# A conditioned hybrid decoder layer on one core: opening in a new order with a fifth weight buffer, conditioning units pinned in DVE's queue, tanh of the branch gates grouped by table

## The chip, the cores and the metric

One Trainium2 chip, and of it one core. The core has five engines with a queue each: PE (TensorE, matmuls), DVE (VectorE), ACT (ScalarE), POOL (GpSimd) and SP (SyncE, here only for issuing DMAs). Each queue runs in order; engines wait for each other by semaphores. The metric is device time in microseconds (us) of one execution, and the median of several runs is compared. A second measure is the span of one profiled execution, from which all rows come.

## What is computed

One layer of a decoder on 256 tokens of width 2048, in float32:

```python
def reference(x, c, w_ada, b_ada, norm1_g, w_in, ...):
    c_act = jax.nn.silu(c)
    mod = jnp.dot(c_act, w_ada[l]) + b_ada[l]
    shift1, scale1, gate1, shift2, scale2, gate2 = jnp.split(mod, 6, axis=-1)
    h = _modulate(_rms_norm(x, norm1_g[l]), shift1, scale1)
    proj = jnp.einsum("bsd,de->bse", h, w_in[l])
    lru_x, lru_gate, q, k, v, g_a, g_b = jnp.split(proj, split_idx, axis=-1)
    xc = _causal_depthwise_conv(lru_x, conv_w[l], conv_b[l])
    rec = _rg_lru(xc, ...)
    y_a = jnp.einsum("bsw,wd->bsd", rec * jax.nn.gelu(lru_gate, approximate=True), w_lru_out[l])
    att = _swa_sink_attention(q, k, v, attn_sinks[l], rel_bias)
    y_b = jnp.einsum("bsw,wd->bsd", att, w_attn_out[l])
    merged = jax.nn.sigmoid(g_a) * y_a + jax.nn.sigmoid(g_b) * y_b
    x = x + gate1[:, None, :] * jnp.einsum("bsd,de->bse", merged, w_out[l])
    h2 = _modulate(_rms_norm(x, norm2_g[l]), shift2, scale2)
    ff = jnp.square(jax.nn.relu(jnp.einsum("bsd,df->bsf", h2, w_ff1[l])))
    x = x + gate2[:, None, :] * jnp.einsum("bsf,fd->bsd", ff, w_ff2[l])
    return _rms_norm(x, final_g)
```

Two things matter here. The input of the first projection, h, needs the first columns of `mod`, and these need the whole conditioning vector times rows of `w_ada`. And the branch gates are sigmoids, which the kernel computes as a tanh of half the argument.

## The kernel before

**Layout.** Activations stand transposed: 16 k-tiles of 128 channels by 256 tokens. Each float32 weight tile of 1 MB (128 x 2048) is fetched by SP into one of four `raw` buffers (`RAW_BUFS`). It is used in halves of 1024 columns: ACT rounds a half to `wh` (L161), DVE computes the remainder `wl` (L163), and each operand pair is multiplied by three matmuls (L177 to L179), or two wide ones (L190, L191). There are three buffers each of `wh` and `wl` (`WH_BUFS`), so one and a half tiles are prepared ahead. A few tiles are multiplied unsplit (L206). Activation pairs, each 128 x 512 floats, come from a pool `kp` of 49 buffers: the x tiles `xs`, the split `h`, the results `res`, and later the split operands. PSUM has four banks for matmul groups (`pg`) and four for all else (`pa`).

**Conditioning.** `mod` has 96 columns of 128 channels. A unit of conditioning (`ada_unit`, L277) is one DVE instruction (L287): it multiplies a `raw` buffer of `w_ada` (1 MB, fetched by SP at L272) with the silu'd vector laid out in a line, `scr`, and sums to one column. The first 32 units are shift1 and scale1, in pairs by k-tile: two units, then `norm1_tile` (L299) makes h[j], with L301 on DVE, L303 and the rounding L146 on ACT, and the remainder L147 on DVE.

**The opening.** Token-major x is fetched in four DMAs (L99) into `wh` and `wl` buffers, `vec` (all small vectors) and the identity `idt` by ACT's queue (L91, L93). PE lays out `scr` by 16 transposes (L225), ACT copies it (L226), ACT and DVE sum squares of x (L229, L233). Then x is scaled by quarters q (`turn_in`, L252): token block 0 on DVE (L254), block 1 on ACT (L255); PE transposes it (L261), ACT copies it to `xs` (L263). Quarter q yields k-tiles 4q to 4q + 3. The order is written out by hand in L307 to L323.

**Passes.** The first projection runs in three passes (`PASSES`: k-tiles 0 to 1 and 2 to 5 for 56 features, 6 to 9 for 40), so that matmuls can begin with two k-tiles done. After each weight tile about 0.85 units of conditioning follow (`ADA_FIRST`). In pass one the results leave PSUM by ACT (L372), in the others they are added by DVE (L374, L376).

**Units.** After that, 240 loop turns (L799) each take one weight tile: the turn splits the weights of two turns ahead, issues its matmuls and what finishes them, then some steps of a list `side` (attention, LRU, gelu) by a budget, then units of conditioning by a budget. Tiles of the rest of the first projection (`in_unit`, L418) are shorter, with 6 or 10 k-tiles a feature. LRU steps come in groups of four: sigmoids (L580, L581), exp and tanh (L587, L588), sqrt (L596), each DVE work between them. The helper `table` (L465) keeps such groups apart: every activation of a group is placed behind all those of the group before, so that ACT's function tables are loaded once a group. The tanh of branch gates (L637, L640) is not among them in this version.

**What sets the order.** A planner orders the instructions on each queue by the program's order and by when it takes their inputs to be ready; an instruction later in the program can be placed earlier. `keep_in_program_order` (called `pin` in the code) ties an instruction to stand behind the last one that the program has issued on the same engine so far; it doesn't wait for that one to finish. The opening is pinned on DVE, ACT and SP, and so are the eight conditioning units 4 to 11.

Of the kernel before, what the change touches and what calls it, by code (L numbers as in the profile page):

```python
# [10 lines left out]
F32 = mybir.dt.float32  # L11
F32R = mybir.dt.float32r
AF = mybir.ActivationFunctionType
ALU = mybir.AluOpType
# [3 lines left out]
P = 128  # L18
# [8 lines left out]
F_K, F_V, F_Q, F_LX, F_LG, F_GA, F_GB = 0, 2, 4, 20, 36, 52, 68  # L27
W_IN_ORDER = (list(range(48, 50)) + list(range(50, 52)) + list(range(32, 48)) + list(range(0, 16))
              + list(range(16, 32)) + list(range(52, 68)) + list(range(68, 84)))
RAW_BUFS, WH_BUFS, WCH = 4, 3, 1024  # L30
LAG, CC, CG, CV, CS = 2, 1, .6, .3, 2.5
SSD = 4

# [7 lines left out]
PASSES = [(0, 2, 56), (2, 6, 56), (6, 10, 40)]  # L41
# [6 lines left out]
def _done(f):  # L48
# [4 lines left out]
V_BADA, V_G1, V_CW, V_CB, V_BA, V_BX, V_LAM, V_G2, V_GF, V_C, V_SINK = (  # L53
    0, 96, 112, 176, 192, 208, 224, 240, 256, 272, 288)
# [4 lines left out]
def hybrid_layer(ctx: ExitStack, tc: tile.TileContext, x, xt, wada, w_p, w_r, w_f, vec, lruw, relb,  # L59
                 onehot, maskc, ident, out):  # L60
    nc = tc.nc
    te, ve, se = nc.tensor, nc.vector, nc.scalar

    cp = ctx.enter_context(tc.tile_pool(name="cp", bufs=1))
    wp = ctx.enter_context(tc.tile_pool(name="wp", bufs=2))
    kp = ctx.enter_context(tc.tile_pool(name="kp", bufs=49))
    tp = ctx.enter_context(tc.tile_pool(name="tp", bufs=9))
    sp = ctx.enter_context(tc.tile_pool(name="sp", bufs=2))
    pg = ctx.enter_context(tc.tile_pool(name="pg", bufs=4, space=PSUM))
# [5 lines left out]
    def nm(s):  # L75
        cnt[0] += 1
        return f"{s}{cnt[0]}"

    def pair(dt=F32):
        return kp.tile([P, 2, T], dt, tag="k2", name=nm("k"))  # L80

    def tmp(shape=(P, 2, T), dt=F32):
        return tp.tile(list(shape), dt, tag="t2", name=nm("t"))

    def bank(shape):
        return pa.tile(list(shape), F32, tag="pa", name=nm("pa"))


    pin = tc.keep_in_program_order
    vc = cp.tile([P, NV], F32, name="vc")  # L90
    pin(se.dma_start(out=vc, in_=vec))  # L91
    idt = cp.tile([P, P], F32, name="idt")
    pin(se.dma_start(out=idt, in_=ident))  # L93

    xtok = {}
# [11 lines left out]
    def rstd_cols(ss, pin=lambda i: i):  # L107
        st = sp.tile([P, 8], F32, tag="st", name=nm("st"), bufs=2)
        v, s, r, q = st[:, 0:2], st[:, 2:4], st[:, 4:6], st[:, 6:8]
        pin(ve.tensor_scalar(out=v, in0=ss, scalar1=1.0 / 2048, scalar2=EPS, op0=ALU.mult, op1=ALU.add))  # L110
        pin(se.activation(s, v, AF.Sqrt))
        pin(ve.reciprocal(out=r, in_=s))

        pin(ve.scalar_tensor_tensor(out=q, in0=r, scalar=-0.5, in1=r, op0=ALU.mult, op1=ALU.mult))
        pin(ve.tensor_tensor(out=q, in0=q, in1=v, op=ALU.mult))
        pin(ve.scalar_tensor_tensor(out=r, in0=q, scalar=1.5, in1=r, op0=ALU.add, op1=ALU.mult))
        return r
# [25 lines left out]
    def split(src, pin=lambda i: i):  # L143

        hl = pair(F32R)
        pin(se.activation(hl[:, 0], src, AF.Copy))  # L146
        pin(ve.tensor_tensor(out=hl[:, 1], in0=src, in1=hl[:, 0].bitcast(F32), op=ALU.subtract))  # L147
        return hl


    def w_dma(src, n, pin=lambda i: i):
        raw = wp.tile([P, 2048], F32, tag="raw", name=nm("rw"), bufs=RAW_BUFS)
        pin(nc.sync.dma_start(out=raw[:, :n], in_=src))
        return raw, n

    def w_split(raw, n, pin=lambda i: i, o0=0):
        parts = []
        for o in range(o0, o0 + n, WCH):
            c = min(WCH, o0 + n - o)
            wh = wp.tile([P, WCH], F32R, tag="wh", name=nm("wh"), bufs=WH_BUFS)  # L160
            pin(se.activation(wh[:, :c], raw[:, o:o + c], AF.Copy))  # L161
            wl = wp.tile([P, WCH], F32R, tag="wl", name=nm("wl"), bufs=WH_BUFS)
            pin(ve.tensor_tensor(out=wl[:, :c], in0=raw[:, o:o + c], in1=wh[:, :c].bitcast(F32), op=ALU.subtract))  # L163
            parts.append((wh, wl))
        return parts

    def w_load(src, n):
        return w_split(*w_dma(src, n))
# [48 lines left out]
    scr = cp.tile([P, KT * P], F32, name="scr")  # L217
# [31 lines left out]
    rs1 = rstd_cols(ss1, pin)  # L249
    xs = []  # L250

    def turn_in(q):  # L252

        pin(ve.tensor_scalar(out=xtok[0, q], in0=xtok[0, q], scalar1=rs1[:, 0:1], scalar2=None, op0=ALU.mult))  # L254
        pin(se.activation(xtok[1, q], xtok[1, q], AF.Copy, scale=rs1[:, 1:2]))  # L255
        for j in (2 * q, 2 * q + 1):
            px = bank([P, 512])
            for i in range(2):
                for b in range(2):
                    e = (2 * (j % 2) + i) * P  # L260
                    te.transpose(px[:, i * T + b * P:i * T + (b + 1) * P], xtok[b, q][:, e:e + P], idt)  # L261
            xs.append(pair())
            pin(se.activation(xs[j].rearrange("p a b -> p (a b)"), px, AF.Copy))  # L263
# [4 lines left out]
    same = lambda i: i  # L268

    def ada_dma(pin=same):  # L270
        raw = wp.tile([P, KT * P], F32, tag="raw", name=nm("ra"), bufs=RAW_BUFS)
        pin(nc.sync.dma_start(out=raw, in_=wada[ada_next[0] + len(ada_raw)]))  # L272
        ada_raw.append(raw)

    ada_raw = []

    def ada_unit(pin=same):  # L277
        if not ada_raw:
            ada_dma()
        raw = ada_raw.pop(0)  # L280
        n = ada_next[0]
        ada_next[0] += 1
        c = ADA_ORDER[n]

        if 2 * PASSES[0][1] <= n < 2 * PASSES[0][1] + 8:
            pin = tc.keep_in_program_order
        pin(ve.tensor_tensor_reduce(out=raw, in0=raw, in1=scr, scale=1.0, scalar=vc[:, V_BADA + c:V_BADA + c + 1],  # L287
                                    op0=ALU.mult, op1=ALU.add, accum_out=mod[:, c:c + 1]))
        return n

    h = [None] * KT
    a1 = cp.tile([P, KT], F32, name="a1")

    def ada_norm1():
        n = ada_unit()
        if n % 2 == 1:
            norm1_tile(n // 2)

    def norm1_tile(j, pin=same):  # L299
        xj = xs[j // 2][:, j % 2]  # L300
        pin(ve.scalar_tensor_tensor(out=a1[:, j:j + 1], in0=mod[:, KT + j:KT + j + 1], scalar=1.0,  # L301
                                    in1=vc[:, V_G1 + j:V_G1 + j + 1], op0=ALU.add, op1=ALU.mult))
        pin(se.activation(xj, xj, AF.Identity, scale=a1[:, j:j + 1], bias=mod[:, j:j + 1]))  # L303
        h[j] = split(xj, pin)


    ada_dma(pin)  # L307
    ada_dma(pin)
    first_raw = w_dma(w_p[0], 2048, pin)
    ada_dma(pin)  # L310
    turn_in(0)
    turn_in(1)
    ada_unit(pin)
    n1 = ada_unit(pin)
    first_w = w_split(first_raw[0], WCH, pin)
    norm1_tile(n1 // 2, pin)
    ada_dma(pin)
    ada_unit(pin)
    first_w += w_split(first_raw[0], WCH, pin, WCH)
    n1 = ada_unit(pin)  # L320
    turn_in(2)
    norm1_tile(n1 // 2, pin)
    turn_in(3)  # L323


# [37 lines left out]
    res = {}  # L363
# [37 lines left out]
    while ada_next[0] < 2 * KT:  # L401
        ada_norm1()
# [12 lines left out]
    def later(cost, fn, *a):  # L415
        side.append((cost, fn, a))
# [212 lines left out]

    bg = [None]  # L630

    def branch_gate(f, ps, part):
        if part is None:
            if f % 2 == 0:
                bg[0] = pair()
            res[f] = bg[0][:, f % 2]
            se.activation(res[f], ps, AF.Tanh, scale=0.5)  # L637
        else:
            ve.tensor_tensor(out=part, in0=ps, in1=part, op=ALU.add)
            se.activation(part, part, AF.Tanh, scale=0.5)  # L640


    att, mg = {}, {}
# [135 lines left out]
    in_units(F_LX, 16, lx_fin)  # L779
    in_units(F_LG, 16, lg_fin)  # L780
    in_units(F_GA, 16, lambda f, ps, part: branch_gate(F_GA + f, ps, part))
    in_units(F_GB, 16, lambda f, ps, part: branch_gate(F_GB + f, ps, part))
    n_ya = len(units)
    n_z = n_ya + 32 + Z_FROM
# [153 lines left out]
```

## Time and profile before

| | |
|---|---|
| median of 3 runs | 1591.97 us (1588.78 to 1592.4) |
| the profiled execution, its own time | 1585.86 us |
| its span | 1584.1 us |
| PE busy | 1543.9 us (97%) |
| DVE busy | 1216.9 us (77%) |
| ACT busy | 890.9 us (56%) |
| conditioning units, L287 | 96 of 2.35 us |
| splits, L161 and L163 | 534 each |
| HBM read | 384.13 MB, 244 GB/s over the span |

The span is what the profiler sees of the core from the first to the last instruction; the execution's own time has 1.76 us around it. A busy PE doesn't say that it runs at full rate, but its idle time is real. The rows that the argument needs stand in the prediction: a table of busy time by stretch, the timeline of the opening, and the waits of PE.

### The profile page before, as it was taken

What the parts mean: (1) busy time and instruction counts of PE and PEld (TensorE: products, weight loads), DVE (VectorE), ACT (ScalarE), POOL (GpSimd) and SP (SyncE); (2) the same over time, 40 slices, a digit from 0 to 9 for tenths busy, and PEclk for the clock granted to TensorE, in tenths of its full rate; (3) what the DMA queues carried; (4) which work ended last, traced back from release to release, by engine and by line L of the source; (5) the groups of instructions that cost most, each with busy time, mean ns of one, the idle gap of its engine ahead of it and who ended that gap; (6) DMA issues with size and microseconds to landing.
All of it is one profiled execution on the core that took longest, in us unless ns stands there. A gap on an engine that the chain in (4) does not pass through costs nothing.

```text
span 1584.1 us, 24932 instructions
## 1 busy us (share of the span) xinstructions
PE 1543.9 (97%) x9812; PEld 1383.8 (87%) x9812; DVE 1216.9 (77%) x1941; ACT 890.9 (56%) x1510; POOL 0.2 (0%) x4
## 2 busy tenths in 40 slices
PE   4999999999999999999999999999999999999997
PEld 4999998899988888888889988888888888888886
DVE  5898998898989879788898877965665556655664
ACT  5733447687796564445455863356434663356553
POOL 0000000000000000000000000000000000000000
PEclk7999999999999999999999999999999999999999
DMA  8998976557767768777886666875555555555552
GB/s 324 343 341 321 337 277 210 204 181 242 282 247 291 266 240 301 283 292 288 322 313 239 229 247 249 331 256 190 194 192 189 190 186 186 186 186 188 188 188 75
DMA packets 61126, 387.90 MB, mean 245 GB/s; under 512 B 6512, under 2 KB 10960, under 8 KB 18640
## 3 DMA queue, kind: packets, MB, share of 16 engines
q1 hardware_dynamic: 55728, 380.66, 66.1%
q10 hardware_dynamic: 5280, 5.64, 1.2%
q8 instruction: 77, 1.26, 0.3%
q14 instruction: 41, 0.34, 0.1%
HBM read 384.13 MB, written 2.15 MB: 244 GB/s over the span
## 4 chain that ended last, share of the span: by engine, by line
PE 86%; DVE 5%; DMA 4%; issue 3%; ACT 2%; ACTq 0%; DVEq 0%
PE pg L191 41%; PE pg L190 20%; PE pg L179 5%; PE pg L177 5%; PE pg L178 5%; DMA ra<-in_wada_dram 3%; DVE wl L163 2%; PE pg L206 2%; PE pg L193 1%; PE pg L727 1%; PE pg L728 1%; PE pg L726 1%; DVE ra L287 1%; PE pa L532 1%; PE pa L539 1%
## 5 line engine op out<-in xcount | busy, mean ns | idle before, releaser
L191 PE MATMUL pg<-k,wh 128*128 128x512 f32 x3120 | 1076.0, 394 | 0.3 <-DVE k L147 0.3
L163 DVE TENSOR_TENSOR wl<-rw,wh 128x1024 fp32r<-128x1024 f32 (+2 forms) x534 | 628.3, 1179 | 266.1 <-ACT wh L161 259.8
L161 ACT ACTIVATE wh<-rw 128x1024 fp32r<-128x1024 f32 (+2 forms) x534 | 545.0, 1022 | 509.0 <-PE pg L191 353.3
L190 PE MATMUL pg<-k,wl 128*128 128x256 f32 x2925 | 818.9, 280 | 0.6 <-DVE wl L163 0.6
L191 PEld LDWEIGHTS pg<-k,wh 128*128 128x128 f32 x3120 | 572.6, 188 | 118.9 <-PE pg L191 0.6
L190 PEld LDWEIGHTS pg<-k,wl 128*128 128x128 f32 x2925 | 550.3, 188 | 10.4 <-DVE wl L163 0.9
L177 PE MATMUL pg<-k,wh 128*128 128x256 f32 x832 | 237.6, 287 | 7.4 <-ACT k L146 5.7
L179 PE MATMUL pg<-k,wl 128*128 128x256 f32 x832 | 233.6, 284 | 3.6 <-DVE wl L163 3.6
L287 DVE CUSTOM_DVE_ANT_0 ra<-ra,scr,vc 128x2048 f32<-128x2048 f32 x96 | 225.1, 2346 | 14.4 <-DMA ra<-in_wada_dram 14.3
L178 PE MATMUL pg<-k,wh 128*128 128x256 f32 x832 | 234.2, 282 | 0.0
L177 PEld LDWEIGHTS pg<-k,wh 128*128 128x128 f32 x832 | 157.5, 190 | 10.0 <-ACT k L146 6.5
L179 PEld LDWEIGHTS pg<-k,wl 128*128 128x128 f32 x832 | 156.5, 189 | 6.2 <-DVE wl L163 4.9
L178 PEld LDWEIGHTS pg<-k,wh 128*128 128x128 f32 x832 | 157.5, 189 | 0.7 <-issue 0.3
L754 DVE SCALAR_TENSOR_TENSOR k<-pg,mod,k 128x256 f32<-128x256 f32 x128 | 61.9, 484 | 31.7 <-PE pg L191 29.5
L743 ACT ACTIVATE t<-t 128x256 f32<-128x256 f32 x55 | 23.0, 419 | 68.0 <-DVE t L198 67.8
L193 PE MATMUL pg<-k,wl 128*128 128x256 f32 x195 | 54.7, 281 | 2.0 <-DVE wl L163 2.0
L198 DVE TENSOR_TENSOR t<-pg,t 128x256 f32<-128x256 f32 x131 | 54.8, 418 | 0.0
L197 ACT ACTIVATE t<-pg 128x256 f32<-128x256 f32 x131 | 47.8, 365 | 1.7 <-PE pg L191 1.7
L193 PEld LDWEIGHTS pg<-k,wl 128*128 128x128 f32 x195 | 36.6, 188 | 10.8 <-DVE wl L163 2.8
L727 PE MATMUL pg<-z,wh 128*128 128x256 f32 x144 | 41.0, 285 | 0.0
L726 PE MATMUL pg<-z,wh 128*128 128x258 f32 x144 | 40.7, 282 | 0.0
L728 PE MATMUL pg<-z,wl 128*128 128x258 f32 x144 | 40.6, 282 | 0.0
(161 smaller groups left out, 963.1 us busy)
## 6 DMA issues: line engine op xcount, KB each, us to landing
rw<-in_w_f_dram SPq DMA_DIRECT2D x204, 1024.0 KB, 4.8
ra<-in_wada_dram SPq DMA_DIRECT2D x96, 1024.0 KB, 6.2
rw<-in_w_p_dram SPq DMA_DIRECT2D x31, 1024.0 KB, 6.4
rw<-in_w_r_dram SPq DMA_DIRECT2D x20, 768.0 KB, 4.5
rw<-in_w_r_dram SPq DMA_DIRECT2D x16, 640.0 KB, 3.9
bt<-ud ACTq DMA_DIRECT2D x8, 512.0 KB, 4.0
lw<-in_lruw_dram SPq DMA_DIRECT2D x4, 512.0 KB, 5.9
k<-in_x_dram SPq DMA_DIRECT2D x8, 256.0 KB, 6.0
```

Source lines behind the costliest of these rows:

```text
L161: pin(se.activation(wh[:, :c], raw[:, o:o + c], AF.Copy))
L163: pin(ve.tensor_tensor(out=wl[:, :c], in0=raw[:, o:o + c], in1=wh[:, :c].bitcast(F32), op=ALU.subtract))
L177: te.matmul(ps, lhsT=wh[:, w], rhs=hl[:, 0], start=k == 0, stop=False)
L178: te.matmul(ps, lhsT=wh[:, w], rhs=hl[:, 1], start=False, stop=False)
L179: te.matmul(ps, lhsT=wl[:, w], rhs=hl[:, 0], start=False, stop=k == n - 1)
L190: te.matmul(ps[:, 0], lhsT=wl[:, w], rhs=hl[:, 0], start=False, stop=False)
L191: te.matmul(ps, lhsT=wh[:, w], rhs=hl, start=k == 0, stop=k == n - 1)
L193: te.matmul(ps[:, 0], lhsT=wl[:, w], rhs=hl[:, 0], start=False, stop=False)
L287: pin(ve.tensor_tensor_reduce(out=raw, in0=raw, in1=scr, scale=1.0, scalar=vc[:, V_BADA + c:V_BADA + c + 1], op0=ALU.mult, op1=ALU.add, ac ...
L726: te.matmul(ps, lhsT=wh[:, e], rhs=z[k][:, 0:258], start=k == 0, stop=False)
L727: te.matmul(ps[:, 0:256], lhsT=wh[:, e], rhs=z[k][:, 258:514], start=False, stop=False)
L754: ve.scalar_tensor_tensor(out=x1[f], in0=ps[:, i], scalar=mod[:, 5 * KT + f:5 * KT + f + 1], in1=x1[f], op0=ALU.mult, op1=ALU.add)
```

## The change

It has five parts. `vec` is fetched by SP, ahead of x, so that ACT's queue begins with the identity. `raw` has five buffers instead of four and `kp` 48 instead of 49. The opening has a new order: two conditioning tiles, a weight tile and two conditioning tiles are fetched; quarter 1 is scaled before the first units, but transposed only after h[0]'s rounding; the first half's rounding on ACT comes ahead of h[0], its remainder on DVE behind h[0]'s L301; and h[1] comes ahead of quarters 2 and 3. All conditioning units are pinned on DVE, not only eight. The tanh of branch gates goes through `table` in the group "exp", and that of the four gates begun in pass one is put on the side list.

```diff
-RAW_BUFS, WH_BUFS, WCH = 4, 3, 1024
+RAW_BUFS, WH_BUFS, WCH = 5, 3, 1024
...
-    kp = ctx.enter_context(tc.tile_pool(name="kp", bufs=49))
+    kp = ctx.enter_context(tc.tile_pool(name="kp", bufs=48))
...
-    pin(se.dma_start(out=vc, in_=vec))
+    pin(nc.sync.dma_start(out=vc, in_=vec))
...
+    def w_round(raw, o, c, pin=lambda i: i):
+        wh = wp.tile([P, WCH], F32R, tag="wh", name=nm("wh"), bufs=WH_BUFS)
+        pin(se.activation(wh[:, :c], raw[:, o:o + c], AF.Copy))
+        return wh
+
+    def w_rest(raw, o, c, wh, pin=lambda i: i):
+        wl = wp.tile([P, WCH], F32R, tag="wl", name=nm("wl"), bufs=WH_BUFS)
+        pin(ve.tensor_tensor(out=wl[:, :c], in0=raw[:, o:o + c], in1=wh[:, :c].bitcast(F32), op=ALU.subtract))
+        return wh, wl
...
-    def turn_in(q):
-
-        pin(ve.tensor_scalar(out=xtok[0, q], in0=xtok[0, q], scalar1=rs1[:, 0:1], scalar2=None, op0=ALU.mult))
-        pin(se.activation(xtok[1, q], xtok[1, q], AF.Copy, scale=rs1[:, 1:2]))
+    def turn_in(q, step=None):
+
+        if not step:
+            pin(ve.tensor_scalar(out=xtok[0, q], in0=xtok[0, q], scalar1=rs1[:, 0:1], scalar2=None, op0=ALU.mult))
+            pin(se.activation(xtok[1, q], xtok[1, q], AF.Copy, scale=rs1[:, 1:2]))
+        if step is False:
+            return
...
-    def ada_unit(pin=same):
+    def ada_unit():
...
-        if 2 * PASSES[0][1] <= n < 2 * PASSES[0][1] + 8:
-            pin = tc.keep_in_program_order
-        pin(ve.tensor_tensor_reduce(out=raw, in0=raw, in1=scr, scale=1.0, scalar=vc[:, V_BADA + c:V_BADA + c + 1],
+        tc.keep_in_program_order(ve.tensor_tensor_reduce(out=raw, in0=raw, in1=scr, scale=1.0, scalar=vc[:, V_BADA + c:V_BADA + c + 1],
...
         pin(se.activation(xj, xj, AF.Identity, scale=a1[:, j:j + 1], bias=mod[:, j:j + 1]))
-        h[j] = split(xj, pin)
+        h[j] = pair(F32R)
+        pin(se.activation(h[j][:, 0], xj, AF.Copy))
+
+    def norm1_rest(j, pin=same):
+        xj = xs[j // 2][:, j % 2]
+        pin(ve.tensor_tensor(out=h[j][:, 1], in0=xj, in1=h[j][:, 0].bitcast(F32), op=ALU.subtract))
...
     ada_dma(pin)
     ada_dma(pin)
     first_raw = w_dma(w_p[0], 2048, pin)
     ada_dma(pin)
+    ada_dma(pin)
     turn_in(0)
-    turn_in(1)
-    ada_unit(pin)
-    n1 = ada_unit(pin)
-    first_w = w_split(first_raw[0], WCH, pin)
-    norm1_tile(n1 // 2, pin)
-    ada_dma(pin)
-    ada_unit(pin)
+    turn_in(1, False)
+    ada_unit()
+    ada_unit()
+    whs = w_round(first_raw[0], 0, WCH, pin)
+    norm1_tile(0, pin)
+    turn_in(1, True)
+    first_w = [w_rest(first_raw[0], 0, WCH, whs, pin)]
+    norm1_rest(0, pin)
+    ada_unit()
     first_w += w_split(first_raw[0], WCH, pin, WCH)
-    n1 = ada_unit(pin)
+    ada_unit()
+    norm1_tile(1, pin)
+    norm1_rest(1, pin)
     turn_in(2)
-    norm1_tile(n1 // 2, pin)
     turn_in(3)
...
+    def gate_tanh(f):
+        table("exp", se.activation(res[f], res[f], AF.Tanh, scale=0.5))
+
...
-            se.activation(res[f], ps, AF.Tanh, scale=0.5)
+            table("exp", se.activation(res[f], ps, AF.Tanh, scale=0.5))
         else:
             ve.tensor_tensor(out=part, in0=ps, in1=part, op=ALU.add)
-            se.activation(part, part, AF.Tanh, scale=0.5)
+            later(0.4, gate_tanh, f)
```

7 lines of the change are left out of this document (2 added, 5 removed).

## The prediction

> **What bounds the kernel now.** I read the stages first: a table of busy time by stretch. Columns: stretch, its length, then busy us and instruction count of PE, PE weight load, DVE, ACT, POOL, then the granted clock, the DMA share and GB/s.
>
> ```profile
> 0.00:14.00 14.00, 4.07 (x20) 3.65 (x20) 5.50 (x22) 7.75 (x16) 0.20 (x4) 1.00 0.86 332
> 14.00:20.00 6.00, 2.86 (x14) 2.05 (x13) 5.08 (x5) 3.85 (x6) 0.00 (x0) 0.53 1.01 404
> 20.00:36.00 16.00, 8.78 (x40) 7.92 (x40) 10.30 (x14) 6.56 (x12) 0.00 (x0) 0.54 0.77 294
> 36.00:110.00 74.00, 72.34 (x551) 69.91 (x552) 62.44 (x78) 44.02 (x89) 0.00 (x0) 1.00 0.91 336
> 225.00:330.00 105.00, 101.26 (x850) 88.58 (x849) 92.37 (x317) 72.70 (x220) 0.00 (x0) 1.00 0.61 212
> 330.00:480.00 150.00, 145.38 (x1026) 136.17 (x1025) 137.04 (x236) 122.23 (x209) 0.00 (x0) 1.00 0.69 246
> 480.00:860.00 380.00, 379.01 (x2187) 332.08 (x2186) 330.08 (x497) 206.18 (x335) 0.00 (x0) 1.00 0.77 284
> 860.00:1560.00 700.00, 699.99 (x4127) 617.78 (x4126) 457.35 (x591) 373.70 (x559) 0.00 (x0) 1.00 0.58 207
> 1560.00:1584.10 24.10, 15.29 (x103) 13.54 (x101) 9.09 (x19) 7.70 (x14) 0.00 (x0) 0.87 0.25 88
> ```
>
> PE is the bound from 36 us on. Its idle time is 9.9 + 3.1 + 7.2 = 20.2 us before 36 us, 1.7 in 36:110, 3.7 in 225:330, 4.6 in 330:480, 1.0 in 480:860, nothing in 860:1560, and 8.8 at the end, which the change does not touch. So the change can take from about 30 us of idle, two thirds of it in the opening. PE's matmul work itself is not changed.
>
> Next, the timeline of all engines up to 36 us, with two pieces (the first and the transposes at 28.41) from the chain that ended last, and the issues of SP. A bracket gives the idle time before an instruction and what ended it.
>
> ```profile
> 1.17 5.71 DMA idt<-in_ident_dram
> 5.41 0.22 ACT L213 ACTIVATE sc<-vc 128x16 f32<-128x16 f32 x1 [2.48 <-DMA vc<-in_vec_dram]
> 8.21 0.69 DVE L229 CUSTOM_DVE_ANT_0 t<-wh 128x512 f32<-128x512 f32 x1 [1.16 <-DMA wh<-in_xt_dram]
> 11.56 0.16 DVE L248 TENSOR_REDUCE ss<-ssq 128x2 f32<-128x8 f32 x1 [1.41 <-ACT t L233]
> 12.99 0.88 DVE L254 TENSOR_SCALAR wh<-wh,st 128x512 f32<-128x512 f32 x2
> 16.05 2.35 DVE L287 CUSTOM_DVE_ANT_0 ra<-ra,scr,vc 128x2048 f32<-128x2048 f32 x1
> 18.25 1.05 ACT L161 ACTIVATE wh<-rw 128x1024 fp32r<-128x1024 f32 x1
> 19.34 1.23 DVE L163 TENSOR_TENSOR wl<-rw,wh 128x1024 fp32r<-128x1024 f32 x1 [0.92 <-ACT wh L161]
> 20.48 0.15 DVE L301 SCALAR_TENSOR_TENSOR a<-mod,vc 128x1 f32<-128x1 f32 x1
> 20.73 0.60 ACT L303 ACTIVATE k<-k,mod,a 128x256 f32<-128x256 f32 x1 [1.42 <-DVE a L301]
> 21.83 0.80 PE L177 MATMUL pg<-k,wh 128*128 128x256 f32 x2 [4.10 <-ACT k L146]
> 25.56 2.35 DVE L287 CUSTOM_DVE_ANT_0 ra<-ra,scr,vc 128x2048 f32<-128x2048 f32 x1
> 28.23 0.15 DVE L301 SCALAR_TENSOR_TENSOR a<-mod,vc 128x1 f32<-128x1 f32 x1
> 28.41 1.96 PE pa L261 x8
> 29.54 0.60 ACT L263 ACTIVATE k<-pa 128x512 f32<-128x512 f32 x1 [6.20 <-PE pa L261]
> 30.89 0.59 ACT L303 ACTIVATE k<-k,mod,a 128x256 f32<-128x256 f32 x1
> 31.98 1.22 PE L177 MATMUL pg<-k,wh 128*128 128x256 f32 x4 [1.62 <-ACT k L146]
> 5.78 12.99 SPq L272 DMA_DIRECT2D ra<-in_wada_dram  x3
> ```
>
> The reader is to see two late tiles. h[0] starts PE at 21.83. The second conditioning unit ends at 16.05 + 2.35 = 18.4, but L301 stands in DVE's queue behind the split weight L163 and comes only at 20.48. h[1] starts PE again at 31.98. Its L301 is done at 28.38, but ACT is held by two copies (L263) that wait for transposes, and these wait for DVE's scaling behind the fourth conditioning unit, so L303 starts at 30.89. And SP's third issue of L272 hangs for a weight buffer: the DMA share falls to 0.77 in 20:36.
>
> **The change part by part.**
>
> *The head.* vec goes to SP ahead of x, so idt is alone on ACT's queue. It is 64 KB (128 x 128 x 4 bytes) and took 5.71 us behind 176 KB of vec. If it lands 1.5 to 2.5 us earlier, PE's sixteen transposes and ACT's squares move up; the reduction at 11.56 waited 1.41 us for ACT, and x itself lands at 8.21, so 1.3 us is the most that it brings; nothing, if idt is no earlier. x's four issues each slip by one issue on SP, in a time in which nothing has landed yet. I take 1.3 us at DVE, worth 0.5 us at h[1] (below).
>
> The Trainium skill, "DMA: Bandwidth & Descriptors", section "Issuing engines are not separate DMA queues", speaks against this step: a second issuing engine saves only the issue time, since all queues share the same 16 engines. By it idt would gain only the place of one issue, well under 1 us, and the sum below would be about 0.3 us less; the 5.71 us for 64 KB, late behind 176 KB in one queue, speak for the larger value.
>
> *h[0].* L301 no longer waits for L163, and ACT rounds the first weights before the copies of the second quarter. So L301 comes at about 18.4 instead of 20.48: PE, which followed L303 by 1.1, starts 2.1 us earlier, up to 3.4 with the head. This alone brings nothing at the end: with one of two k-tiles and four PSUM banks PE runs 12 matmuls and stops again.
>
> *h[1].* On DVE, after L301 at 18.4: L163 (1.14 us to the next start, 19.34 to 20.48), L147 as PE's first matmul, by about 19.9, then a unit of 2.35 less some 0.1 that neighbours overlap, the second half's split 1.14, a unit again: L301 at 25.5 instead of 28.23. L303 now follows at once (25.7 instead of 30.89), because quarters 2 and 3 come behind it: 5.2 us. Data: SP has five buffers, so the first four units and the first weights are all issued at the start. From the stage table 4.65 MB have come by 14 us and 0.404 MB per us after; vec, idt and x are 2.34 MB and each tile 1.05 MB, so the third unit lands at about 18.7 and the fourth at 21.3, both before DVE wants them. These landings let only a part of the head's 1.3 us through, and I add 0.5: h[1] 5.7 us earlier, at about 26.3.
>
> *What moves behind it.* Quarter 2's eight transposes took 1.96 us in PE's idle time at the granted clock of 0.54; now they stand on PE's path: 1.0 us at full clock to 2.0 us at half. Its two copies (0.6 each) and a scaling on ACT also delay the next weights' rounding, which waits until quarter 3's transposes free the buffer. I charge 1.4. **Opening: 5.7 - 1.4 = 4.3 us**, bounds 2.0 (h[0]'s gain only) and 5.7.
>
> *Does it last?* DVE and ACT are shifted with PE. DMA has to be as well: 36:110 runs at 0.91. In 20:36 it left 0.23 x 16 = 3.7 us unused, for want of a buffer; the fifth fills this. So supply moves up by about as much as PE.
>
> *The fifth buffer later.* Rows of the first pass change:
>
> ```profile
> 78.16 2.00 ACT L161 ACTIVATE wh<-rw 128x1024 fp32r<-128x1024 f32 x2 [2.91 <-DMA rw<-in_w_p_dram]
> 81.87 0.38 PE L179 MATMUL pg<-k,wl 128*128 128x256 f32 x1 [0.74 <-DVE wl L163]
> ```
>
> Here a weight tile arrived late and cost PE 0.74 us (its own idle; the stretch 36:110 lost 1.7 in all). One issue slot earlier is some 2.6 us (1.05 MB at 0.404). I take 0.7 back; bounds 0 and 1.7. One activation buffer fewer (48): I count at most 48 pairs in use at the gates (16 h, 32 results), so a pair is free when its successor is asked for: nothing, but if wrong a copy waits for one matmul group.
>
> *Conditioning units pinned.* The three largest waits of PE after 110 us, with the conditioning unit on DVE that stood ahead of the awaited split each time, and for the middle one ACT's rounding of those weights:
>
> ```profile
> 359.05 2.35 DVE L287 CUSTOM_DVE_ANT_0 ra<-ra,scr,vc 128x2048 f32<-128x2048 f32 x1
> 362.60 0.39 PE L179 MATMUL pg<-k,wl 128*128 128x256 f32 x1 [1.68 <-DVE wl L163]
> 383.93 1.05 ACT L161 ACTIVATE wh<-rw 128x1024 fp32r<-128x1024 f32 x1
> 384.66 2.35 DVE L287 CUSTOM_DVE_ANT_0 ra<-ra,scr,vc 128x2048 f32<-128x2048 f32 x1
> 388.55 0.39 PE L179 MATMUL pg<-k,wl 128*128 128x256 f32 x1 [0.97 <-DVE wl L163]
> 440.78 2.35 DVE L287 CUSTOM_DVE_ANT_0 ra<-ra,scr,vc 128x2048 f32<-128x2048 f32 x1
> 444.91 0.39 PE L193 MATMUL pg<-k,wl 128*128 128x256 f32 x1 [1.97 <-DVE wl L163]
> ```
>
> At 384.98 the rounded weights were ready, but DVE had begun a unit of 2.35 us 0.3 us before. A pinned unit stands behind the last DVE instruction of its loop turn, a join or a side step that itself waits for PE or ACT, so it can no longer slip ahead there. The three waits make 1.68 + 0.97 + 1.97 = 4.6 us, PE's whole idle time in 330:480; all of it back is one bound. The other: a pin adds a wait. Behind a waiting unit stand the next weights' L163 and the joins that free PSUM, and for these PE waits. DVE is 91% busy in 330:480, so a unit of 2.35 us has to stand ahead of something: the same three waits again, 0 back, or three new ones, 4.6 lost.
>
> *Tanh by table.* In program order tanh now alternates with the last two LRU groups: I count 12 loads where the trace has 10 (below the first and the last, with two activations between), since a tanh must wait for the sqrt traced before it and the next sqrt for that tanh.
>
> ```profile
> 428.67 1.28 ACT L596 ACT_TABLE_LOAD   x1
> 429.96 0.42 ACT L596 ACTIVATE t<-t 128x256 f32<-128x256 f32 x1
> 452.47 0.41 ACT L637 ACTIVATE k<-t 128x256 f32<-128x256 f32 x1
> 477.67 1.28 ACT L637 ACT_TABLE_LOAD   x1
> ```
>
> Two loads at 1.28 are 2.6 us of ACT, which is 81% busy in 330:480; the tanh at 452.47 needed none, between sigmoids. I charge half, 1.3 us; bounds 0 and, with all eight units of that stretch held up, 8 x 1.97 = 15.8.
>
> The Trainium skill, "ScalarE: Activation LUTs", section "What ACT_TABLE_LOAD costs", puts a switch at 1.28 us and a drain of 1.38 more. By it the two loads would cost 5.3 us of ACT, and the sum would be 1.3 us worse; the row has no drain: the activation at 429.96 starts 1.29 us after the load's start.
>
> **Sum.** 4.3 + 0.7 + 4.6 - 1.3 = 8.3 us. The profiled execution is 1585.86 us (span 1584.1), so 1577.6 for such a one. The median before is 1591.97, 6.1 above it, over runs from 1588.78 to 1592.4; the terms do not depend on that, so I take the difference off the median: **1583.7 us**.
>
> **The rivals.**
>
> *Supply takes the opening back.* DMA stays at its 36:110 rate and the first late weight at 78 us lands when it did; PE, 4.3 us early, then waits longer there. For: 0.91 busy. Against: the unused 3.7 us, and the fifth buffer. Left are the later terms, 3.3 us, and little of the opening: 1588.
>
> *The pins move the waits instead of removing them.* For: DVE at 91% and short units there. Against: the row of 384.66. Left are 4.3 + 0.7 - 1.3 = 3.7 us: 1588.3.
>
> *Slower: tanh and sqrt chained to PE.* Place: the eight units at 428:478. The sqrt of each next LRU step waits for a tanh, which waits for that unit's join, and ACT's queue holds the next rounding behind it. Price: up to 1.97 us a unit, as at 444.91. It decides from four units on, where 7.9 us eat the opening and the fifth buffer and the pins bring nothing; with all eight 15.8 + 1.3 - 5.0 = 12.1 slower, with six about 8: 1600. Against: the order of the trace is already nearly that one.
>
> *More.* h[1]'s whole 5.7, all of 1.7 and 4.6, no tanh charge: 12.0 us, 1580.
>
> **How the numbers follow.** Forecast 0.48 (1581 to 1586.5), more 0.12, supply 0.14, moved waits 0.17, slower or a new wait of its size 0.09. A measurement of this kernel can tell about 0.3% (4.8 us, so 1587.2 and 1596.7) from no change. The two middle rivals lie just inside it, with a fifth of their chance beyond on the fast side, and 0.02 of the last stays within: faster 0.66, same 0.27, slower 0.07. The range is 1576 to 1592: the fast case less the 3.2 us by which the runs before spread downwards, and to the median before, so that about 0.1 is left above and less below.
>
> **What would show it.** Right: PE's first L177 at 18.5 to 19.8 and the second group at 25 to 27, DMA share above 0.9 in 20:36, idt landed before 5.4, PE idle before 36 us of 14 to 16 us; no PE wait over 1 us after a unit in 330:480. Wrong: PE waits for weights at 65 to 90 us of over 2 us in all, or more PE idle than 4.6 us in 330:480.

## The result: slower, and the profile after

The changed kernel takes 1610.06 us (median of 4 runs, 1608.37 to 1610.76), against 1590.38 us for the kernel before on the same chip: ratio 1.0123, 95% interval 1.0104 to 1.0143. The forecast was 1583.7 us, faster, with a range of 1576 to 1592.

Line numbers shift: the split pair is now L158 and L163, the narrow matmuls L183 to L185 (before L177 to L179), the unsplit ones L212 (L206), a conditioning unit L294 (L287), the last add of a pass L393 (L376), h[j]'s rounding and remainder L313 and L317 (L146, L147), its inputs L309 and L311 (L301, L303), scaling L261 and L262, transposes L270, their copies L272. First the stages, in the columns and stretches of before:

```profile
0.00:14.00 14.00, 3.81 (x17) 3.44 (x17) 5.33 (x21) 7.84 (x16) 0.20 (x4) 1.00 0.85 312
14.00:20.00 6.00, 3.85 (x16) 2.95 (x16) 5.25 (x7) 3.35 (x6) 0.00 (x0) 1.00 1.03 431
20.00:36.00 16.00, 9.15 (x45) 8.53 (x46) 11.72 (x14) 8.88 (x19) 0.00 (x0) 1.00 1.01 420
36.00:110.00 74.00, 70.15 (x526) 68.07 (x525) 57.34 (x73) 40.87 (x85) 0.00 (x0) 0.98 0.78 302
110.00:225.00 115.00, 113.13 (x897) 110.22 (x897) 106.70 (x164) 45.68 (x54) 0.00 (x0) 1.00 0.88 322
225.00:330.00 105.00, 95.19 (x785) 83.95 (x783) 84.06 (x296) 62.73 (x189) 0.00 (x0) 0.97 0.56 193
330.00:480.00 150.00, 146.11 (x1042) 134.65 (x1041) 134.29 (x242) 117.05 (x210) 0.00 (x0) 1.00 0.67 237
480.00:860.00 380.00, 376.19 (x2141) 327.71 (x2140) 329.44 (x478) 214.55 (x354) 0.00 (x0) 1.00 0.77 284
860.00:1560.00 700.00, 697.48 (x4114) 615.02 (x4114) 458.96 (x614) 370.66 (x558) 0.00 (x0) 1.00 0.59 211
```

Length less PE's busy time is its idle time. Before 36 us it fell from 20.2 to 19.2. In 36:110 it grew from 1.7 to 3.9, in 110:225 from 0.1 to 1.9, in 225:330 from 3.7 to 9.8, in 480:860 from 1.0 to 3.8, in 860:1560 from nothing to 2.5; of the stretches behind 36 us only 330:480, where the pins were to help, fell, from 4.6 to 3.9. DVE is less busy in 36:110 than before (57.3 against 62.4 us): it did not become the bound by work, it stood still more. The clock column is not to be read before 36 us: it shows 1.00 there, but the matmuls from 21.6 to 32.3 us start 0.21 us apart, as those of the kernel before did where it showed 0.54; from 35.4 us on they start 0.12 us apart.

Over the profiled execution (1609.78 us, span 1608.0) PE is also busy for longer:

```profile
PE 1554.8 (97%) x9812; PEld 1389.6 (86%) x9812; DVE 1218.7 (76%) x1941; ACT 891.9 (55%) x1512; POOL 0.2 (0%) x4
```

1554.8 against 1543.9 us, for the same matmuls. So of 23.9 us of span, 13.0 are idle PE and 10.9 are longer busy time. Of these 1.1 stand before 36 us. Behind 36 us, the share of the clock that was not granted, summed over stretches of 8 us, makes 9.5 us after and 3.2 before, so by this estimate some 6 of the 10.9 are a lower clock; the rest was not told apart. The table of waits, PE alone, 36 to 330 us (total us, times, longest), says for what PE waits; its first line for the split, before and after:

```profile
PE pg L179 <- DVE wl L163: 0.9, 2, 0.7
```

```profile
PE pg L185 <- DVE wl L163: 10.5, 6, 3.2
```

The longest but one of the six, in the timeline (start, duration, engine, line; in brackets the idle time before and what ended it):

```profile
73.60 1.99 ACT L158 ACTIVATE wh<-rw 128x1024 fp32r<-128x1024 f32 x2
73.73 0.42 DVE L317 TENSOR_TENSOR k<-k,k 128x256 fp32r<-128x256 f32 x1 [1.14 <-ACT k L313]
76.26 0.85 DVE L393 TENSOR_TENSOR k<-pg,k 128x256 f32<-128x256 f32 x2 [2.11 <-PE pg L212]
77.56 0.42 DVE L393 TENSOR_TENSOR k<-pg,k 128x256 f32<-128x256 f32 x1 [0.44 <-PE pg L212]
79.28 0.42 DVE L393 TENSOR_TENSOR k<-pg,k 128x256 f32<-128x256 f32 x1 [1.30 <-PE pg L212]
79.62 2.34 DVE L294 CUSTOM_DVE_ANT_0 ra<-ra,scr,vc 128x2048 f32<-128x2048 f32 x1
81.89 2.36 DVE L163 TENSOR_TENSOR wl<-rw,wh 128x1024 fp32r<-128x1024 f32 x2
83.17 0.39 PE L185 MATMUL pg<-k,wl 128*128 128x256 f32 x1 [2.90 <-DVE wl L163]
```

The adds L393 wait for PE, and DVE idles 2.11 + 0.44 + 1.30 = 3.9 us. The unit is pinned behind the last of them. It begins when that add is done, although the next weights had been rounded since 75.6, and their two splits stand behind it for 2.3 us. PE, which from 78.87 to 80.26 multiplied what needs only the rounded weights and now needs the remainder `wl`, waits 2.90 us. Then it runs at half rate for a while (windows of the same kernel, columns as above):

```profile
80.00:83.10 3.10, 0.26 (x2) 0.06 (x1) 3.10 (x4) 0.00 (x0) 0.00 (x0) 1.00 0.86 299
83.10:87.00 3.90, 3.83 (x20) 3.83 (x20) 1.57 (x3) 0.00 (x0) 0.00 (x0) 0.58 0.99 395
87.00:90.00 3.00, 3.00 (x26) 3.00 (x26) 2.62 (x4) 1.44 (x2) 0.00 (x0) 0.98 0.58 232
```

The granted clock is 0.58 in the 3.9 us after the wait: 20 matmuls, where at the rate of the next stretch (26 in 3.0) there would be 34. That is part of the 10.9.

### The profile page after: what moved, and what is told of

It is laid out like the page before. It is cut to its first block, busy times and chain, and to the rows that moved or that the text cites. A ratio compares the mean times of both kernels' runs of the same rounds, so it can differ in the third digit from the quotient of the medians.

```text
span 1608.0 us, 24927 instructions
## 1 busy us (share of the span) xinstructions
PE 1554.8 (97%) x9812; PEld 1389.6 (86%) x9812; DVE 1218.7 (76%) x1941; ACT 891.9 (55%) x1512; POOL 0.2 (0%) x4
## 4 chain that ended last, share of the span: by engine, by line
PE 85%; DVE 8%; ACT 3%; issue 2%; DMA 1%; SPq 0%; ACTq 0%; DVEq 0%
PE pg L197 43%; PE pg L196 21%; PE pg L185 4%; PE pg L183 4%; PE pg L184 4%; DVE ra L294 3%; DVE wl L163 3%; PE pg L212 2%; PE pg L199 1%; ACT wh L158 1%; PE pg L747 1%; PE pg L748 1%; PE pg L746 1%; DMA rw<-in_w_p_dram 1%; PE pa L556 1%
## 5 line engine op out<-in xcount | busy, mean ns | idle before, releaser
L163 DVE TENSOR_TENSOR wl<-rw,wh 128x1024 fp32r<-128x1024 f32 (+2 forms) x534 | 626.6, 1177 | 278.5 <-ACT wh L158 273.1
L158 ACT ACTIVATE wh<-rw 128x1024 fp32r<-128x1024 f32 (+2 forms) x534 | 544.3, 1022 | 526.8 <-PE pg L197 362.1
L185 PE MATMUL pg<-k,wl 128*128 128x256 f32 x832 | 236.9, 287 | 11.8 <-DVE wl L163 11.7
L183 PE MATMUL pg<-k,wh 128*128 128x256 f32 x832 | 238.9, 289 | 9.6 <-ACT k L313 6.5
L294 DVE CUSTOM_DVE_ANT_0 ra<-ra,scr,vc 128x2048 f32<-128x2048 f32 x96 | 224.6, 2341 | 0.0
L185 PEld LDWEIGHTS pg<-k,wl 128*128 128x128 f32 x832 | 159.0, 192 | 14.6 <-DVE wl L163 13.7
L183 PEld LDWEIGHTS pg<-k,wh 128*128 128x128 f32 x832 | 159.2, 192 | 13.3 <-ACT k L313 7.2
L199 PEld LDWEIGHTS pg<-k,wl 128*128 128x128 f32 x195 | 36.6, 188 | 10.9 <-DVE wl L163 2.9
```

The lines of the kernel that those rows point to most:

```text
L183: te.matmul(ps, lhsT=wh[:, w], rhs=hl[:, 0], start=k == 0, stop=False)
L185: te.matmul(ps, lhsT=wl[:, w], rhs=hl[:, 0], start=False, stop=k == n - 1)
L199: te.matmul(ps[:, 0], lhsT=wl[:, w], rhs=hl[:, 0], start=False, stop=False)
L294: tc.keep_in_program_order(ve.tensor_tensor_reduce(out=raw, in0=raw, in1=scr, scale=1.0, scalar=vc[:, V_BADA + c:V_BADA + c + 1], op0=ALU. ...
```

## The experiments

Three theories were to be told apart. *Pins*: the pinned unit can't use a gap of DVE and then stands ahead of a split. *Fifth buffer*: a planner with more buffers places units or weights elsewhere. *Tanh*: the grouped tanh chains ACT. Lines are those of the changed kernel unless another is named; each ratio is to the kernel before in the same batch.

**1. Pins taken away.** From unit 12 on none is pinned.

```diff
-        tc.keep_in_program_order(ve.tensor_tensor_reduce(out=raw, ...
+        (tc.keep_in_program_order if n < 12 else same)(ve.tensor_tensor_reduce(out=raw, ...
```

> The changed kernel with units of conditioning pinned only up to unit 11, as before the change. If the pins cost the time (a unit of 2.35 us that waits behind a join for PE and then stands ahead of the next split), the execution falls from 1610 to 1580 to 1592 us and PE's waits for wl of 1 us and more before 320 us go. If the tanh order or the opening with five buffers costs it, it stays at 1604 to 1611.

1589.34 us, 1.0010 (0.9995 to 1.0025): 1.13 of the 1.23% are gone, some 18 us. The same place in its timeline:

```profile
72.44 2.35 DVE L294 CUSTOM_DVE_ANT_0 ra<-ra,scr,vc 128x2048 f32<-128x2048 f32 x1
74.71 0.42 DVE L317 TENSOR_TENSOR k<-k,k 128x256 fp32r<-128x256 f32 x1
79.22 0.42 DVE L393 TENSOR_TENSOR k<-pg,k 128x256 f32<-128x256 f32 x1 [1.30 <-PE pg L212]
79.56 2.35 DVE L163 TENSOR_TENSOR wl<-rw,wh 128x1024 fp32r<-128x1024 f32 x2
80.83 0.39 PE L185 MATMUL pg<-k,wl 128*128 128x256 f32 x1 [0.75 <-DVE wl L163]
```

The unit went into the gap ahead of the adds, the splits follow the last add at once, and PE waits 0.75 us.

**2. The kernel before with the pins alone.**

```diff
-        if 2 * PASSES[0][1] <= n < 2 * PASSES[0][1] + 8:
+        if n >= 2 * PASSES[0][1]:
```

> The kernel before with every unit from 4 on pinned, nothing else. If the pins cost the time by themselves, 1604 to 1616 us (18 us more, and somewhat more where only four buffers hold the tiles that a waiting unit keeps). If they cost it only together with the new opening or the tanh order, 1588 to 1595.

1615.45 us, 1.0176 (1.0155 to 1.0196). Pins alone bring more than the whole loss, 26.5 us, with four buffers and the old opening. The same line of its waits, 36 to 330 us:

```profile
PE pg L179 <- DVE wl L163: 16.6, 12, 3.1
```

**3. Tanh as before** (the two `table`/`later` lines undone), and **4. tanh and pins both undone**, which leaves the opening, the fifth buffer and 48 pairs.

```diff
-            table("exp", se.activation(res[f], ps, AF.Tanh, scale=0.5))
+            se.activation(res[f], ps, AF.Tanh, scale=0.5)
...
-            later(0.4, gate_tanh, f)
+            se.activation(part, part, AF.Tanh, scale=0.5)
```

> The changed kernel with the tanh of the branch gates outside the table groups, as before the change. If the tanh chained to sqrt costs the time, 1588 to 1596 us. If the pins cost it, 1604 to 1611; of the 4 us that are lost between 330 and 600 us up to 4 may return.

1607.09 us, 1.0123 (1.0108 to 1.0139), the same ratio as with the tanh grouped: tanh is not the cause.

> New opening, five buffers, 48 pairs; pins and tanh as before the change. If the opening's 4 us last, 1583 to 1588 us. If the supply takes them back, 1588 to 1592. If the new opening or the buffers themselves upset the order on the queues, over 1595.

1591.61 us, 1.0024 (1.0012 to 1.0036). The parts that were to bring 5.0 us cost 3.8 by the ratio. Runs 7 to 9 take them apart.

**5. Where the pins cost: in the passes only, or after them only** (unit 32 is the first behind the passes).

```diff
+        (tc.keep_in_program_order if n < 2 * KT else same)(...
...
+        (tc.keep_in_program_order if n < 12 or n >= 2 * KT else same)(...
```

> The changed kernel with units pinned only while the three passes run (units 0 to 31). If each pin costs where it stands, the passes' share comes back as it was: the first attention score at 237 to 240 us, as in the changed kernel (239.3), and no further loss behind it, so 1594 to 1599 us. If the later pins alone cost the time, the first score is at 232 and the time 1587 to 1592.

> The changed kernel with units 12 to 31 free and all later ones pinned. If each pin costs where it stands, the first score is at 232 us as with no pins, and the loss of some 8 us comes between 240 and 600 us: 1596 to 1601 us. If the passes' pins alone cost the time, 1587 to 1592.

1598.08 us, 1.0056 (1.0041 to 1.0071), and 1604.31 us, 1.0096 (1.0081 to 1.0111). Against 1.0010 without late pins these are 0.46% (7 us) and 0.86% (14 us), against 18 us for all pins at once: both stages pay. In the kernel with late pins only, PE still waits 6.1 us for remainders between 36 and 330 us, in four waits. Which waits make up the rest of the late part is not shown here.

**6. Is it the join?** From unit 12 on each unit is tied behind the last split issued so far instead of behind the last DVE instruction. That last instruction is mostly a join, an add such as L393 that waits for PE's result; so the unit stays out of the way of the splits but need not wait for a join.

```diff
-        tc.keep_in_program_order(ve.tensor_tensor_reduce(out=raw, ...
+        (tc.keep_in_program_order if n < 12 else behind_split)(ve.tensor_tensor_reduce(out=raw, ...
```

> The changed kernel with each unit from 12 on tied behind the last split of weights that the program has issued (in a pass that of the same tile, later that of two turns ahead), instead of behind the last instruction on DVE, which is mostly a join that waits for PE. If the wait for the join is the cost, nearly all comes back: 1584 to 1593 us. If any tie that takes the planner's freedom to fill DVE's gaps costs, 1600 or more.

1599.05 us, 1.0065 (1.0048 to 1.0082): half of the pins' price comes back, which lies between the two expectations. In the passes nearly all does: PE's first score matmul starts at 233.8 us, at 239.3 with pins and 232.0 without. Some 4 of the 9 us that are left stand at one place (lines of this kernel: L302 is the unit, L165 the split):

```profile
590.52 2.35 DVE L302 CUSTOM_DVE_ANT_0 ra<-ra,scr,vc 128x2048 f32<-128x2048 f32 x1
592.79 1.22 DVE L165 TENSOR_TENSOR wl<-rw,wh 128x1024 fp32r<-128x1024 f32 x1
594.26 3.10 DVE L147 TENSOR_TENSOR k<-k,k 128x256 fp32r<-128x256 f32 x9
594.82 0.76 PE L199 MATMUL pg<-k,wh 128*128 128x512 f32 x1 [4.05 <-DVE k L147]
```

Here the unit, with a split behind it, keeps back the remainders of activations (L147) that PE needs, so at this place the tie only moves the victim.

**7. Fifth buffer and 48 pairs in the kernel before**, and **8. 48 pairs alone**.

```diff
-RAW_BUFS, WH_BUFS, WCH = 4, 3, 1024
+RAW_BUFS, WH_BUFS, WCH = 5, 3, 1024
-    kp = ctx.enter_context(tc.tile_pool(name="kp", bufs=49))
+    kp = ctx.enter_context(tc.tile_pool(name="kp", bufs=48))
```

> The kernel before with five buffers for tiles and 48 pairs, nothing else. If buffers are no bound in the passes, 1586 to 1591 us. If 48 pairs are short, a wait of PE of 1 us or more for a split activation appears near 905 to 930 us and the time is 1590 to 1594. If the fifth buffer lets the tiles come earlier, the 0.7 us wait at 81 us goes and 1584 to 1588.

> The kernel before with 48 pairs instead of 49, four buffers, nothing else. If the lost pair made the cost of the run with five buffers and 48 pairs (9.6 us), 1595 to 1600 us, with a wait for a split activation near 920 us. If the fifth buffer made it, by letting the planner place units earlier, 1586 to 1591; between the two, the wait near 920 us is the pair's share, about 3 us.

1598.01 us, 1.0054 (1.0039 to 1.0070) with both, 1590.74 us, 1.0010 (1.0001 to 1.0020) with the pair alone. The fifth buffer does harm. The wait for a split activation that was looked for near 920 us is there with both (1.43 us at 929.71) and not with the pair alone. Another of its places, in the run with both:

```profile
263.13 2.35 DVE L287 CUSTOM_DVE_ANT_0 ra<-ra,scr,vc 128x2048 f32<-128x2048 f32 x1 [2.88 <-DMA ra<-in_wada_dram]
269.50 1.22 PE L532 MATMUL pa<-idt,t 128*128 128x128 f32 x6 [2.34 <-DVE as L500]
```

and in the kernel before:

```profile
266.72 1.22 PE L532 MATMUL pa<-idt,t 128*128 128x128 f32 x6 [0.20 <-DVE as L500]
270.49 2.35 DVE L287 CUSTOM_DVE_ANT_0 ra<-ra,scr,vc 128x2048 f32<-128x2048 f32 x1
```

With five buffers the order has a unit ahead of the attention work L500, and DVE stands 2.88 us for that unit's data before it runs; with four the unit comes behind. So a buffer changes the order of DVE's queue, and a waiting filler holds what is behind it. That this accounts for all of the 0.44% between the two runs was not shown.

**9. The opening alone**, with four buffers, 49 pairs, the old pins and tanh; and the same with quarter 2 scaled and transposed ahead of h[1] (below, what the second adds to the first).

```diff
+    turn_in(2, False)
...
+    turn_in(2, True)
...
-    turn_in(2)
```

> The kernel before with the new opening and vec on SP alone: four buffers, 49 pairs, pins and tanh as before. If the opening itself gains what its trace with five buffers showed, the first unsplit matmul (start of pass two) comes at 71.5 to 72.5 us instead of 73.2 and the time is 1585 to 1588 us. If it needs the fifth buffer to feed its first four units, h[1] comes later than 29 us and nothing is gained: 1588 to 1591. Over 1592 if the planner's later order is upset by it.

> As the run before, but quarter 2 is scaled and transposed ahead of h[1], in PE's idle time, as in the kernel before. If the transposes and copies that the new opening puts behind h[1] are what takes its gain, the start of pass two comes 1 to 2.5 us earlier than in the run before (69.5 to 71 us). If something else does (supply, DVE), it comes within 0.5 us of it.

1588.16 us, 1.0000 (0.9990 to 1.0009), and 1587.37 us, 0.9995 (0.9986 to 1.0004). The opening's gain can't be measured at the end. At the start of pass two it is small: the first unsplit matmul starts at 73.2 us before, at 72.7 and 71.2 in these. Single profiles spread here by more than a microsecond. In the four of this document with the old opening the start lies at 73.2 to 74.5, in the eleven with the new one at 71.2 to 73.1, in the five with quarter 2 first at 69.5 to 72.0. So the new opening is about 2 us ahead there, and quarter 2 first perhaps 1 more.

**10. Is it the wait or the unit's length?** Each unit sums 512 columns instead of 2048, pinned and free.

```diff
-        ...(out=raw, in0=raw, in1=scr, scale=1.0, ...
+        ...(out=raw[:, :512], in0=raw[:, :512], in1=scr[:, :512], scale=1.0, ...
```

> The changed kernel, but every unit of conditioning sums only 512 of its 2048 columns (this part of the result is left out), so that it holds DVE for about 0.7 us instead of 2.35; all fetches and pins stay. If a pin costs because a unit of 2.35 us stands between the join and the next split, this runs within 5 us of the next run, which has no pins. If the pin costs through its wait or the lost freedom of order, it stays 12 us or more above it.

> The changed kernel with the same short units and pins only up to unit 11. 1572 to 1586 us by either theory; it is the base for the run before.

1582.52 us, 0.9971 (0.9960 to 0.9983), and 1584.08 us, 0.9971 (0.9962 to 0.9980): with short units the pins cost nothing. In the pinned run:

```profile
78.35 0.42 DVE L393 TENSOR_TENSOR k<-pg,k 128x256 f32<-128x256 f32 x1 [1.30 <-PE pg L212]
78.69 0.74 DVE L294 CUSTOM_DVE_ANT_0 ra<-ra,scr,vc 128x512 f32<-128x512 f32 x1
79.36 2.36 DVE L163 TENSOR_TENSOR wl<-rw,wh 128x1024 fp32r<-128x1024 f32 x2
80.63 0.39 PE L185 MATMUL pg<-k,wl 128*128 128x256 f32 x1 [1.42 <-DVE wl L163]
```

The order is that of the changed kernel, unit behind the last add and ahead of the splits. At this place only the unit's length differs, by 1.6 us, and PE waits 1.42 instead of 2.90 us. In 82.5:84.5 of this run the granted clock is 1.00. Over the whole kernel, though, the short units also take 139 us of work off DVE (1079.7 us busy for 1218.7), so these two runs don't separate the length of one unit from DVE's load.

**11. Units in two halves.** Two instructions of 1024 columns each, the first pinned, the second free; as a measure of the halving itself the kernel of 9 (quarter 2 first) with both halves free.

```diff
+            f(ve.tensor_tensor_reduce(out=raw[:, :1024], ..., accum_out=vc[:, V_BADA + c:V_BADA + c + 1]))
+            ve.tensor_tensor_reduce(out=raw[:, 1024:], ..., accum_out=mod[:, c:c + 1])
```

> The changed kernel, but from unit 12 on each unit is two instructions of 1024 columns (about 1.25 us each): the first pinned, the second free behind it. The result is whole. If what a pin costs is the time for which the pinned unit stands ahead of the next split, half of the 20 us goes if the planner puts splits between the halves, a third or less if it doesn't: 1595 to 1604. If the length has nothing to do with it, 1608 to 1614.

> A candidate: the kernel before with the new opening, quarter 2 ahead of h[1], and units from 12 on in two free halves; four buffers, 49 pairs, no further pins, tanh as before. If a unit's length on DVE is what PE's waits at 360, 388 and 445 us come from, these shrink to under 1 us each and the time is 1580 to 1586 us. If the planner just puts both halves in one gap, 1586 to 1590; DVE's extra start of some 0.1 us a unit is hidden.

1606.79 us, 1.0109 (1.0093 to 1.0126), and 1596.00 us, 1.0045 (1.0030 to 1.0059). Halving alone costs 0.5% against 0.9995, and so it can't be read from these whether it relieves a pin: inconclusive.

**12. Tanh grouped on the kernel of 9** (quarter 2 first).

> A candidate: the new opening with quarter 2 ahead of h[1] and the tanh by table, with four buffers, 49 pairs and the old pins. If the tanh order by itself helps (with five buffers and no pins it was 2.3 us faster, with pins 3 us slower), 1583 to 1587 us. If it only shifts the planner's order one way or the other, 1585 to 1592.

1589.52 us, 1.0000 (0.9991 to 1.0009) against 0.9995 (0.9986 to 1.0004): no difference.

**13. Units placed elsewhere on the kernel of 9** (quarter 2 first): none in turns with short tiles, and a lower rate throughout.

```diff
-            ada_credit += size / 2048 * ADA_RATE
+            ada_credit += (size == 2048) * ADA_RATE
...
-LOOK, CREDIT, Z_FROM, ADA_RATE, ADA_FIRST = 2, 2.3, 12, 0.45, 0.85
+LOOK, CREDIT, Z_FROM, ADA_RATE, ADA_FIRST = 2, 2.3, 12, 0.2, 0.85
```

> A candidate: the new opening with quarter 2 ahead of h[1] (four buffers, 49 pairs, old pins, old tanh), and no units of conditioning in the loop turns with short tiles (before some 425 us); they are made up for later, in the turns of the output projections, where DVE has more room. If a unit of 2.35 us ahead of a split is what PE's waits between 225 and 425 us come from, those at 361 and 388 us go and the time is 1580 to 1585 us. If the later turns lose as much, 1586 to 1590.

> The same with units at less than half the rate (0.2 a full tile instead of 0.45) in all turns before the output projections. By the same reason fewer waits in proportion: 1583 to 1587 us; no gain (1586 to 1590) if the planner puts the remaining units where they hurt.

1594.43 us, 1.0037 (1.0022 to 1.0051), and 1603.88 us, 1.0095 (1.0078 to 1.0112). Both missed: moved out of one stage, the units make PE wait in another. PE's idle time in 330:480 falls from 5.4 us (the kernel of 9, quarter 2 first) to 2.1 and 2.5, but in 480:860 it rises from 0.4 to 5.6 and 9.5. Of the versions with whole units none is measurably faster than the kernel before.

## Why the prediction was wrong

**The step that failed** is "Conditioning units pinned", and in it the bounds: "the same three waits again, 0 back, or three new ones, 4.6 lost". It was entered at +4.6 us. Runs 1 and 2 give 18 us lost beside the other parts and 26.5 alone. What it said of 330:480 held in part: no wait of over 1 us there is for a split (one of 1.3 us is for ACT's rounding), and the idle time fell to 3.9. But only three waits, where a free unit had collided with a split, were priced. Newly pinned are units 12 to 95, 84 of them, and as free units most had done no harm that PE's waits show: they filled time in which DVE waits for others, as at 72.44 us in run 1. The prediction names that very wait ("a join or a side step that itself waits for PE or ACT") and what stands behind the unit, and then prices it only in 330:480, where DVE is 91% busy and has few gaps. In the first passes, where a pass's last adds wait for PE, a gap was there to lose.

**The price of such a wait** was also short. The matmuls after it can run at half rate for more than 3 us, as behind 83.17, and this was nowhere in the sum.

**The rival "the pins move the waits"** had the mechanism but put its price at the loss of the gain, 1588.3. The rival for slower looked at the tanh, which cost nothing that can be measured.

**Fifth buffer, +0.7 (0 to 1.7).** Outside its bounds, and the wrong mechanism: 0.54% slower with the 48 pairs in the kernel before, 0.24% (run 4 against run 9) beside the new opening. The wait at 81.87 us was not for supply. The weights that landed late were rounded by 80.16 (78.16 + 2.00), and the splits stand behind an add that waits for PE; rows of the kernel before:

```profile
80.26 0.42 DVE L376 TENSOR_TENSOR k<-pg,k 128x256 f32<-128x256 f32 x1 [0.86 <-PE pg L206]
80.60 2.35 DVE L163 TENSOR_TENSOR wl<-rw,wh 128x1024 fp32r<-128x1024 f32 x2
```

With five buffers and no pins (run 1) this wait is still 0.75 us. The 48 pairs cost 0.1%, at the limit of what was measured.

**Opening, +4.3 (2.0 to 5.7).** The mechanism was right, three terms were mis-sized. The timeline after:

```profile
3.78 3.68 PE L231 MATMUL pa<-idt,sc 128*128 128x128 f32 x16 [3.78 <-DVE sc L220]
9.78 0.69 DVE L235 CUSTOM_DVE_ANT_0 t<-wh 128x512 f32<-128x512 f32 x1 [2.43 <-DMA wh<-in_xt_dram]
13.28 0.88 DVE L261 TENSOR_SCALAR wh<-wh,st 128x512 f32<-128x512 f32 x2
18.52 1.06 ACT L158 ACTIVATE wh<-rw 128x1024 fp32r<-128x1024 f32 x1 [1.40 <-DMA rw<-in_w_p_dram]
18.74 0.16 DVE L309 SCALAR_TENSOR_TENSOR a<-mod,vc 128x1 f32<-128x1 f32 x1
20.57 1.01 PE L183 MATMUL pg<-k,wh 128*128 128x256 f32 x3 [1.85 <-ACT k L313]
27.08 0.60 ACT L311 ACTIVATE k<-k,mod,a 128x256 f32<-128x256 f32 x1 [4.64 <-DVE a L309]
28.18 0.80 PE L183 MATMUL pg<-k,wh 128*128 128x256 f32 x2 [4.66 <-ACT k L313]
30.21 0.60 ACT L272 ACTIVATE k<-pa 128x512 f32<-128x512 f32 x1 [1.47 <-PE pa L270]
35.31 0.39 PE L183 MATMUL pg<-k,wh 128*128 128x256 f32 x1 [1.62 <-ACT k L389]
```

The head gained nothing at DVE: idt came in time, but the second half of x landed 1.6 us later (9.78 for 8.21), and the scaling starts at 13.28 instead of 12.99. In all sixteen profiles with vec on SP the scaling starts at 12.15 to 14.57, in the four without at 12.99 to 13.40, so no gain of 1.3 us can be counted on. h[0]'s rounding now stands behind that of the first weights, which landed only at 18.52: PE starts at 20.57, not 18.5 to 19.8. So h[1] is 3.8 us earlier (28.18 for 31.98), not 5.7. And the charge behind it was 2.9, not 1.4: from h[1] to the next group PE took 7.1 us (28.18 to 35.31) instead of 4.3 (31.98 to 36.24). Quarter 2's transposes alone took 1.9 us of it (29.09 to 31.03), at the slow rate. What is left, 0.9 us, agrees with 1.0 at pass two's start in this pair of profiles (72.2 for 73.2); over all profiles it is about 2 us (run 9), half of the forecast and its lower bound. PE's idle time before 36 us is 19.2, not 14 to 16. The DMA share in 20:36 is 1.01, as forecast; no gain from it shows: with four buffers (run 9) pass two starts within the same spread.

**Tanh, -1.3.** Twelve loads were counted:

```profile
L613 ACT ACT_TABLE_LOAD x7 | 9.0, 1283 | 0.1
L657 ACT ACT_TABLE_LOAD x5 | 6.4, 1283 | 0.1
```

There are twelve (groups by line; busy us and mean ns of one), two more than before. Run 4, with five buffers and the old tanh, has fourteen, so the number follows the planner's order too. The grouped tanh costs nothing measurable beside the pins (run 3) or without them (run 12); run 1 is 0.14% below run 4, within their intervals. ACT is 78% busy in 330:480 (117.05 of 150), so that it has room for them.

The sign that was to show the forecast wrong, "PE waits for weights at 65 to 90 us of over 2 us in all", is the row at 83.17.

## What to carry to other kernels

A long filler on an in-order queue earns its place by being free: a pin behind an instruction that waits for another engine can turn the filler's length into delay for what comes next, so before pinning count the gaps that it fills now, stage by stage, and not only the places where it collides. Length matters too: pinned units of 2.35 us cost 18 us in all, units of 0.74 us nothing, though these also left DVE with less work. And one buffer more is also another order: look at what the planner puts first once it may ask for data earlier.

## What the runs showed of the hardware

**A wait of PE of a few microseconds can halve the matmul rate, and the length of one wait doesn't decide it.** After 2.90 us of idle PE the granted clock fell to 0.58 for 3.9 us (windows above), and after 3.18 us (at 253.51 in the changed kernel) it is 0.50 in 255.4:257.4. Shorter waits went both ways. After 1.84 us (505.52, changed kernel) it is 0.50 in 508:510 and after 1.42 us (926.13, run 1) 0.50 in 928:930; after 1.97 us (444.91, the kernel before) it is 1.00 up to 450, and after the 1.42 us of run 10 it is 1.00. What else decides it was not tested. The Trainium skill, "TensorE: Matmul & The Clock Gate", section "What's actually happening", puts the drop at an idle window of about 3.4 us whose phase is free; here shorter waits sufficed. A mean of 0.58 over 3.9 us is half rate for 3.3 us, close to the 3.4 us that the page gives for coming back.

**A small transfer came sooner when it did not stand behind a larger one.** idt, 64 KB, landed 5.7 to 6.1 us after its issue in the four profiles in which it stands behind vec in ACT's queue, and 2.7 to 2.9 us after it in the sixteen in which it is alone there. vec, 176 KB, itself landed after 2.5 to 2.7 us on SP ahead of x, instead of 4.7. The head did not gain: x's second half reaches DVE at 8.70 to 11.07 us instead of 8.21 to 8.52. Queue and order ahead of x changed together, so these runs don't say which of the two did it.
